# Modulation vectors in blocks of 256 features, layer 1's amid the first feed-forward part, with a third buffer for turned probabilities and the first pair's loads on Pool's queue

## The chip, the cores and the metric

The kernel runs on one core of a Trainium2 chip. The engines are PE (TensorE, the matmuls), DVE (VectorE), ACT (ScalarE), POOL (GpSimd) and SP (SyncE, which here issues most of the DMAs); PEld is PE's loading of weights beside its matmuls. Each engine takes its instructions in the order in which they are queued, and waits at an instruction whose data or buffer isn't ready. The metric is the time of one execution on the device in microseconds (us): the median of several runs.

## What is computed

Two layers of a hybrid backbone over 1024 latent tokens and 256 context tokens of 1024 features. Every layer is an attention part and a feed-forward part, each behind a norm whose shift, scale and gate come from the conditioning vectors c and c_ctx.

```python
def _rms(x, g):
    x32 = x.astype(jnp.float32)
    y = x32 * lax.rsqrt(jnp.mean(x32 * x32, axis=-1, keepdims=True) + EPS)
    return (y * g.astype(jnp.float32)).astype(x.dtype)

def _swiglu(h, wg, wu, wd):
    return (jax.nn.silu(h @ wg) * (h @ wu)) @ wd

# layer 0: Fourier groups beside windowed attention with 8 query and 2 key heads
o = jnp.concatenate([_fourier_mix(f), _window_attention(q, k, v, kc, vc, sink)], axis=-1) @ w_out
# layer 1: 2-D neighbourhood attention with 16 heads and a relative bias
o = _neighbourhood_attention(q, k, v, kc, vc, rel_bias) @ w_out
```

The modulation is, for each layer, SiLU of the conditioning vector times a matrix `ada_w` of 1024 x 6144, plus a bias `ada_b`. The 6144 results are six vectors of 1024: shift, scale and gate of the attention part, then of the feed-forward part. There are two rows: one for the latent tokens, one for the context. The inner width of the feed-forward part is 2816, that is, 22 slices of 128.

## The kernel before

Big matmuls are computed with operands that are split into a high and a low part, three matmuls (high x high, low x high, high x low; `mm3`, lines 74 to 76) in place of one. The stages lie on the span about as follows: head and first projection to 200 us, the Fourier part, attention 0 from 236 to 469, output projection and first feed-forward part to 1530, projection of layer 1 to 1870, attention 1 to 2143, then the second output projection and feed-forward part to the end.

**Modulation.** The weights of the first third of layer 0 come in the head, in eight blocks of 256 features (`ada_block`). A block is 1 MB: one load, matmuls with the conditioning vector as the weight side (32 columns) and 256 features moving, four parts of the contraction side by side in PE's column groups (line 126; called M here), ACT's copy of the four partial rows, two small matmuls that add the parts and turn the rows into columns (line 133; called F), and DVE's addition of the bias. The other five thirds (two of layer 0, three of layer 1) run in attention 0 as `ada_third`: eight loads of 1 MB, four matmuls of 512 features for each (line 149), and a finish: ACT copies the rows, four transposes turn them (line 157), and DVE adds the bias. That makes 40 load steps and 5 finishes, spread over the 78 units of attention by a table (`before`), with a PSUM bank of their own (`psa`). The norm gains for layer 1 follow attention 0.

**Attention.** A `Unit` is one block of 128 queries with its keys. `scores` runs the matmuls, `maxima` (DVE) adds the bias and finds the maximum, `exponents` (ACT) writes the probabilities `pr` and their sum, `normalise` scales them (DVE's reciprocal at line 607, then Pool), and `turn` transposes them in parts of 128 keys into PSUM tiles `pt_ps` (PE, line 616), from where DVE (line 622, the first part) or ACT (line 620, the second) copies them to `prob_t`; the matmuls `po` with the values follow. The parts of a unit are at most two or three PSUM banks wide. `pipeline2` (line 630) goes through the units in pairs: the step for pair b emits its scores, normalises pair b-1 and turns pair b-2. Inside attention the order on PE, DVE, ACT and Pool is the one in which the code emits it (`manual_schedule`); in the other stages a scheduler sets it.

**Feed-forward.** `ffn` (line 855) goes through the slices f in blocks of 3, 3, and eight times 2. `gate_up` takes one f over the chunks of tokens (512, the context's 256, and 512; in the text below C0, CX and C1): matmuls `g_ps` and `u_ps` with the two weights, SiLU, product, and the split into act_hi and act_lo. `down` multiplies a block's slices by w_down and adds the result to x. Each weight, 512 KB, passes through `weights` (line 788): a tile `w_raw` of a pool with **two** buffers, loaded by SP; ACT's cast to `w_hi` (line 794), and DVE's difference `w_lo` (line 795); w_hi and w_lo have four buffers each. A buffer of w_raw comes free when both have been computed.

```python
self.ww, self.ww_cm = pools.open(f"weights{l}", bufs=4)
self.wr, self.wr_cm = pools.open(f"raw{l}", bufs=2)
...
raw = self.wr.tile(shape, F32, name="w_raw")
nc.sync.dma_start(raw, raw_ap)
```

**Attention 1** works through 8 pairs of heads. `load_pair` takes k, q and v of a pair from DRAM into a pool with two buffers; `load_part` issues the loads from SP's queue. In the program they come after all writes of the projection (`v_d` last). Pool's queue loads `mask1` (line 1101) at the head of this stage, clears the bias tables `btab` and adds the mask to them (line 1134).

## Time and profile before

| | |
|---|---|
| time, median of 3 runs (lowest, highest) | 2992.25 us (2988.78, 2996.73) |
| the profiled execution | 2993.83 us |
| its span (first to last instruction) | 2991.7 us |
| mean granted clock of PE | 0.989 |
| DVE, ACT, POOL busy | 46%, 29%, 10% of the span |
| loads of the modulation, 1 MB each (`ada_w`) | 48, median 4.9 us from issue to landing |
| loads of k, 640 KB, and q, 512 KB, in layer 1 | median 10.4 and 16.7 us |

How to read the rows further below. A row of the busy windows has the stretch, its length, then for PE, PEld, DVE, ACT and POOL the busy time with the number of instructions, then PE's granted clock (1.00 is full speed), the mean busy share of the DMA engines, and GB/s. A row of instruction groups has the line, engine, operation, output <- inputs, partitions x elements and count; then busy time in us and the mean of one in ns; then the idle time of the engine just before them and what ended it. A row of waits has the engine, the waiting tile and line, what it waited for, the total in us, how many times, and the longest. A row of the timeline has start and length in us, engine, line, operation, and in brackets the idle time before it with its releaser. A row of DMA issues has the tensors, the issuing queue (SPq is SP's), the count, KB each and the median us from issue to landing. PE's matmuls overlap in the pipeline, so the time from start to start is shorter than one row's length.

### The profile page before, as it was taken

What the parts mean: (1) busy time and instruction counts of PE and PEld (TensorE: products, weight loads), DVE (VectorE), ACT (ScalarE), POOL (GpSimd) and SP (SyncE); (2) the same over time, 40 slices, a digit from 0 to 9 for tenths busy, and PEclk for the clock granted to TensorE, in tenths of its full rate; (3) what the DMA queues carried; (4) which work ended last, traced back from release to release, by engine and by line L of the source; (5) the groups of instructions that cost most, each with busy time, mean ns of one, the idle gap of its engine ahead of it and who ended that gap; (6) DMA issues with size and microseconds to landing.
All of it is one profiled execution on the core that took longest, in us unless ns stands there. A gap on an engine that the chain in (4) does not pass through costs nothing.

```text
span 2991.7 us, 37131 instructions
## 1 busy us (share of the span) xinstructions
PE 2854.2 (95%) x14830; PEld 2288.4 (76%) x14830; DVE 1372.8 (46%) x2510; ACT 863.2 (29%) x1637; POOL 308.6 (10%) x435
## 2 busy tenths in 40 slices
PE   7988889999999999999979999699999999999999
PEld 5875547888888888888857788577677888888887
DVE  5774443533223333333575241466564444444446
ACT  4344443421111111111253231466543111111110
POOL 1112222000000000000130001455210000000000
PEclk9989999999999999999999999899999999999999
DMA  7226554211011101110124332877231111111111
GB/s 273 99 100 231 192 196 160 74 36 43 29 43 35 43 31 41 43 42 30 54 92 131 113 104 86 203 175 174 104 105 43 49 43 43 56 43 53 47 43 71
DMA packets 117212, 267.12 MB, mean 89 GB/s; under 512 B 9232, under 2 KB 67088, under 8 KB 110000
## 3 DMA queue, kind: packets, MB, share of 16 engines
q1 hardware_dynamic: 111920, 252.22, 26.8%
q10 hardware_dynamic: 4176, 8.53, 0.8%
q0 software_dynamic: 944, 4.00, 0.4%
q8 instruction: 117, 1.92, 0.3%
q14 instruction: 55, 0.45, 0.0%
HBM read 223.69 MB, written 41.03 MB: 88 GB/s over the span
## 4 chain that ended last, share of the span: by engine, by line
PE 73%; DVE 5%; ACT 2%; issue 2%; DMA 2%; POOL 1%; SPq 0%; POOLq 0%; ACTq 0%; DVEq 0%
PE d_ps L76 9%; PE d_ps L74 9%; PE d_ps L75 9%; PE u_ps L76 7%; PE u_ps L75 7%; PE u_ps L74 7%; PE g_ps L76 7%; PE g_ps L74 7%; PE g_ps L75 7%; PE pt_ps L616 1%; DVE sm L596 1%; PE po L1185 1%; DVE nrm_t L846 1%; ACT pr L602 1%; POOL pr L608 1%
## 5 line engine op out<-in xcount | busy, mean ns | idle before, releaser
L794 ACT CAST w_hi<-w_raw 128x1024 fp32r<-128x1024 f32 x188 | 195.2, 1049 | 888.8 <-PE d_ps L75 489.8
L897 DVE SCALAR_TENSOR_TENSOR x<-d_ps,mod,x 128x512 f32<-128x512 f32 (+1 forms) x400 | 348.1, 881 | 166.3 <-PE d_ps L76 165.4
L795 DVE TENSOR_TENSOR w_lo<-w_raw,w_hi 128x1024 fp32r<-128x1024 f32 x184 | 224.0, 1224 | 300.6 <-ACT w_hi L794 295.9
L881 DVE TENSOR_TENSOR sg<-sg,u_ps 128x512 f32<-128x512 f32 (+1 forms) x110 | 69.8, 634 | 569.5 <-PE u_ps L76 569.5
L74 PE MATMUL d_ps<-act_hi,w_hi 128*128 128x512 f32 (+1 forms) x880 | 327.6, 373 | 3.5 <-DVE x L897 3.4
L75 PE MATMUL d_ps<-act_lo,w_hi 128*128 128x512 f32 (+1 forms) x880 | 327.6, 372 | 1.3 <-DVE act_lo L883 1.3
L76 PE MATMUL d_ps<-act_hi,w_lo 128*128 128x512 f32 (+1 forms) x880 | 327.7, 372 | 0.0
L602 ACT ACTIVATE pr<-sm,st 128x640 f32<-128x640 f32 (+4 forms) x208 | 162.4, 781 | 224.5 <-DVE st L596 201.5
L74 PEld LDWEIGHTS d_ps<-act_hi,w_hi 128*128 128x128 f32 x880 | 165.6, 188 | 37.4 <-DVE x L897 5.6
L608 POOL TENSOR_SCALAR pr<-pr,st 128x640 f32<-128x640 f32 (+2 forms) x208 | 156.0, 750 | 335.6 <-DVE st L607 207.3
L75 PEld LDWEIGHTS d_ps<-act_lo,w_hi 128*128 128x128 f32 x880 | 165.6, 188 | 32.6 <-DVE act_lo L883 1.8
L76 PEld LDWEIGHTS d_ps<-act_hi,w_lo 128*128 128x128 f32 x880 | 165.6, 188 | 31.2
L74 PE MATMUL u_ps<-o_hi,w_hi 128*128 128x512 f32 (+1 forms) x528 | 189.0, 358 | 0.0
L75 PE MATMUL u_ps<-o_lo,w_hi 128*128 128x512 f32 (+1 forms) x528 | 189.0, 358 | 0.0
L76 PE MATMUL u_ps<-o_hi,w_lo 128*128 128x512 f32 (+1 forms) x528 | 188.9, 358 | 0.0
L74 PE MATMUL g_ps<-o_hi,w_hi 128*128 128x512 f32 (+1 forms) x528 | 188.3, 357 | 0.0
L75 PE MATMUL g_ps<-o_lo,w_hi 128*128 128x512 f32 (+1 forms) x528 | 188.2, 357 | 0.0
L76 PE MATMUL g_ps<-o_hi,w_lo 128*128 128x512 f32 (+1 forms) x528 | 188.2, 357 | 0.0
L616 PE MATMUL pt_ps<-ident,pr 128*128 128x128 f32 x944 | 148.4, 281 | 36.0 <-DVE st L607 16.1
L616 PEld LDWEIGHTS pt_ps<-ident,pr 128*128 128x128 f32 x944 | 105.5, 141 | 68.5 <-DVE pt L622 26.5
L829 POOL TENSOR_TENSOR nrm_ss<-nrm_ss,nrm_sq 128x512 f32<-128x512 f32 (+1 forms) x38 | 48.2, 1268 | 1061.6 <-PE d_ps L76 935.7
L882 ACT CAST act_hi<-sg 128x512 fp32r<-128x512 f32 (+1 forms) x110 | 63.6, 578 | 298.0 <-DVE sg L881 298.0
(263 smaller groups left out, 5892.4 us busy)
## 6 DMA issues: line engine op xcount, KB each, us to landing
ada_w<-ada_w SPq DMA_DIRECT2D x48, 1024.0 KB, 4.9
w_raw<-w_gate SPq DMA_DIRECT2D x44, 512.0 KB, 3.4
w_raw<-w_up SPq DMA_DIRECT2D x44, 512.0 KB, 3.4
w_raw<-w_down SPq DMA_DIRECT2D x44, 512.0 KB, 3.5
k<-k_d SPq DMA_DIRECT2D x32, 640.0 KB, 10.4
w_raw<-w_out SPq DMA_DIRECT2D x32, 512.0 KB, 3.5
w_raw<-w_in SPq DMA_DIRECT2D x24, 512.0 KB, 4.5
q<-q_d SPq DMA_DIRECT2D x16, 512.0 KB, 16.7
```

What stands on the lines that cost most here:

```text
L74: TE.matmul(out, lh, rh, start=first, stop=False)
L75: TE.matmul(out, lh, rl, start=False, stop=False)
L76: TE.matmul(out, ll, rh, start=False, stop=last)
L602: S.activation(self.pr[:, :n], self.sm[:, :n], AF.Exp, bias=st[:, 0:1], scale=-1.0, accum_out=st[:, 1:2])
L608: G.tensor_scalar(self.pr[:, :n], self.pr[:, :n], st[:, 3:4], 0.0, ALU.mult, ALU.add)
L616: TE.transpose(pt[:, b * P:(b + 1) * P], self.pr[:, (b0 + b) * P:(b0 + b + 1) * P], ident)
L794: S.copy(hi, raw)
L795: eng.tensor_tensor(lo, raw, fl(hi), ALU.subtract)
L829: adder(i).tensor_tensor(ss, ss, sq, ALU.add)
L881: V.tensor_tensor(sg[:, :n], sg[:, :n], u_ps[:, :n], ALU.mult)
L882: S.copy(a_hi[:, sl], sg[:, :n])
L897: V.scalar_tensor_tensor(xs, self.shaped(ps[:, :n]), vec(l, 5)[:, dt, v:v + 1], xs, ALU.mult, ALU.add)
```

## The change

- The modulation runs in blocks of 256 features everywhere; `ada_third` and its PSUM bank are gone. Layer 0's blocks 8 to 23 run in attention 0, a load ahead, M and F in turn at the beginning of every step of a pair, from the third on. Their PSUM tile is a `pt_ps`.
- Layer 1's 24 blocks run in the first feed-forward part: a generator `modulation1` that `gate_up` advances for f > 1, by two steps behind the first chunk and one behind each of the others. A block is loaded in two halves of 512 KB, into the two buffers of `w_raw`.
- `pst` of attention 0 has three buffers (as attention 1's has had).
- `turn` goes through a unit's parts from the last to the first, so that ACT's copy comes first and DVE's last; `pipeline2` emits maxima, turn, exponents in place of maxima, exponents, turn. Both attentions share this code.
- In attention 1 each of the two buffers for k, q, v is a pool of its own, and the first pair's seven loads are issued from Pool's queue.

```diff
-    def ada_block(b, xpool, wpool, ptr, name):
-        w = xpool.tile([P, KT, 256], F32, name="ada_w", tag="x8")
-        nc.sync.dma_start(w, io["ada_w0"][b])
+    def ada_block(b, xpool, wpool, ptr, name, parts=1, tag="x8"):
+        l, ct = b // 24, 2 * (b % 24)
+        n = KT // parts
+        ws = [xpool.tile([P, n, 256], F32, name="ada_w", tag=tag) for _ in range(parts)]
+        for i, w in enumerate(ws):
+            nc.sync.dma_start(w, io["ada_w"][b, :, i * n:(i + 1) * n])
         yield
         ps = ptr.tile([P, 512], F32, name=name)
         for i in range(2):
             for q in range(4):
-                TE.matmul(ps[32 * q:32 * q + 32, :256], csil[:, 4 * i + q, :], w[:, 4 * i + q],
+                k = 4 * i + q
+                TE.matmul(ps[32 * q:32 * q + 32, :256], csil[:, k, :], ws[k // n][:, k % n],
                           start=i == 0, stop=i == 1, tile_position=(0, 32 * q))
...
         def turn(self):
-            b0 = 0
-            for s0, sl in self.parts:
+            b0 = self.ncol // P
+            for s0, sl in reversed(self.parts):
                 n = (sl.stop - sl.start) // P
+                b0 -= n
...
                 for u in new[i:i + 1]:
                     u.maxima()
-                    u.exponents()
                 for u in turned[i:i + 1]:
                     u.turn()
+                for u in new[i:i + 1]:
+                    u.exponents()
...
-    pst, pst_cm = pools.open("pst", bufs=2, psum=True)
+    pst, pst_cm = pools.open("pst", bufs=3, psum=True)
...
-    psa, psa_cm = pools.open("psa", bufs=1, psum=True)
...
-    steps = [f for l, s_ in ((0, 1), (0, 2), (1, 0), (1, 1), (1, 2))
-             for f in ada_third(l, s_, xq, aw, psa, pst, "pt_ps")]
-    for i, f in enumerate(steps):
-        before.setdefault(i * 78 // len(steps) + 1, []).append(f)
+    def modulation(ada, i):
+        if i % 2 == 0 and i // 2 + 1 < len(ada):
+            advance(ada[i // 2 + 1], 1)
+        advance(ada[i // 2], 1 + i % 2)
+    ada = [ada_block(b, xq, aw, pst, "pt_ps") for b in range(8, 24)]
+    advance(ada[0], 1)
+    for i in range(2 * len(ada)):
+        before.setdefault(2 * (2 + i), []).append(lambda i=i: modulation(ada, i))
...
                     advance(side, 8)
+                    if f > 1:
+                        advance(extra, 2 if c0 == 0 else 1)
...
+    def modulation1():
+        for b in range(24, 48):
+            yield from ada_block(b, dl.wr, dl.wk, dl.pm, "pmisc", 2, "w_raw")
+            yield
+        ada_gain(1, 1, 2)
+        ada_gain(1, 4, 3)
+    steps = dl.ffn(last, fin0, ((CX, C0, C1), norm1, first_weights), modulation1())
...
-    kp, kp_cm = pools.open("kp1", bufs=2)
+    kps, kp_cms = zip(*(pools.open(f"kp1{i}") for i in range(2)))
...
-            nc.sync.dma_start(dst, src)
+            (nc.sync if pr else G).dma_start(dst, src)
```

Where this moves instructions. **SP in the first feed-forward part**, the loads of slices f = 2 to 5 with the first down block between them. Names ending in a number are single tiles; `w_raw` and the half blocks `ada_w` (128 x 1024) share two buffers. Before:

```order
135 L792 DMA w_raw_5791<-w_gate 128x1024
136 L792 DMA w_raw_5797<-w_up 128x1024
137 L792 DMA w_raw_5970<-w_down 128x1024
138 L792 DMA w_raw_5976<-w_down 128x1024
139 L792 DMA w_raw_5982<-w_down 128x1024
140 L792 DMA w_raw_6252<-w_gate 128x1024
```

Now, at the same place:

```order
111 L772 DMA w_raw_5757<-w_gate 128x1024
112 L772 DMA w_raw_5763<-w_up 128x1024
113 L124 DMA ada_w_5826<-ada_w 128x1024
114 L124 DMA ada_w_5827<-ada_w 128x1024
115 L124 DMA ada_w_5955<-ada_w 128x1024
116 L124 DMA ada_w_5956<-ada_w 128x1024
117 L772 DMA w_raw_5959<-w_down 128x1024
118 L772 DMA w_raw_5965<-w_down 128x1024
119 L772 DMA w_raw_5971<-w_down 128x1024
120 L772 DMA w_raw_6241<-w_gate 128x1024
121 L772 DMA w_raw_6247<-w_up 128x1024
122 L124 DMA ada_w_6380<-ada_w 128x1024
```

Each pair of half blocks stands between two pairs of weights, and takes both raw buffers.

**PE at the end of a slice**, with the last `u_ps` of f = 2 and the beginning of the first down block. Before:

```order
2514 L75 MATMUL u_ps_5916<-o_lo_1664,w_hi_5799 128x512
2515 L76 MATMUL u_ps_5916<-o_hi_1663,w_lo_5800 128x512
2516 L74 MATMUL d_ps_5988<-act_hi_5395,w_hi_5972 128x512
2517 L75 MATMUL d_ps_5988<-act_lo_5396,w_hi_5972 128x512
2518 L76 MATMUL d_ps_5988<-act_hi_5395,w_lo_5973 128x512
```

Now:

```order
2505 L76 MATMUL u_ps_5901<-o_hi_1663,w_lo_5766 128x512
2506 L130 MATMUL pmisc_6310<-ada_w_5955,csil_65 32x256 x4
2507 L130 MATMUL pmisc_6310<-ada_w_5956,csil_65 32x256 x4
2508 L137 MATMUL pmisc_6321<-sel_68,ada_rows_6319 128x2 x2
2509 L74 MATMUL d_ps_5977<-act_hi_5361,w_hi_5961 128x512
2510 L75 MATMUL d_ps_5977<-act_lo_5362,w_hi_5961 128x512
2511 L74 MATMUL d_ps_5988<-act_hi_5361,w_hi_5961 128x512
2512 L75 MATMUL d_ps_5988<-act_lo_5362,w_hi_5961 128x512
```

M and F of a block stand between u_ps and d_ps, whose w_hi_5961 is the cast of w_raw_5959, loaded behind the half blocks that M reads. M and F stand together like this at 12 places, six ahead of a down block and six ahead of the next slice's gate; at the other 12 M stands ahead of the last chunk of a slice and F behind it.

**Pool at the start of attention 1.** Before:

```order
221 L1101 DMA mask1_14255<-mask1 128x896
222 L1207 MEMSET btab0_14257 128x256
223 L1207 MEMSET btab1_14258 128x256
224 L1207 MEMSET btab2_14259 128x256
225 L1207 MEMSET btab3_14260 128x256
226 L1128 DMA btab0_14257<-rel_bias 128x512
```

Now:

```order
221 L1092 DMA mask1_14682<-mask1 128x896
222 L1116 DMA k_14689<-k1_d_85 64x2x1280 x4
223 L1116 DMA q_14688<-q1_d_84 64x2x1024 x2
224 L1199 MEMSET btab0_14684 128x256
225 L1199 MEMSET btab1_14685 128x256
226 L1199 MEMSET btab2_14686 128x256
227 L1199 MEMSET btab3_14687 128x256
228 L1120 DMA btab0_14684<-rel_bias 128x512
```

The loads of k and q stand behind the mask's, and the load of v follows those of the bias.

**ACT in attention 0** (`pr` is the exponent's output, `pt` the target of the copy of a turned part). Before:

```order
288 L602 ACTIVATE pr_3157,st_3155<-sm_3153,st_3155 128x641
289 L620 COPY pt_2941<-pt_ps_3164 128x256
290 L602 ACTIVATE pr_3174,st_3172<-sm_3170,st_3172 128x641
291 L620 COPY pt_2941<-pt_ps_3181 128x256
292 L723 CAST o_hi_1663<-po_3112 128x2x128
```

Now:

```order
294 L596 COPY pt_2946<-pt_ps_3153 128x256
295 L577 ACTIVATE pr_3162,st_3151<-sm_3149,st_3151 128x641
296 L596 COPY pt_2946<-pt_ps_3170 128x256
297 L577 ACTIVATE pr_3179,st_3168<-sm_3166,st_3168 128x641
298 L698 CAST o_hi_1663<-po_3110 128x2x128
299 L133 COPY ada_rows_3198<-pt_ps_3189 128x256
```

Within a unit's turn the copy now stands ahead of the exponent, and the copy of a block's rows stands between two steps.

## The prediction, made before the changed kernel was run

> **What bounds the kernel now.** I read the page's busy shares first, then the chain that ended last, then the windows stage by stage, the waits of PE inside each stage, and single steps on the timeline.

> ```profile
> span 2991.7 us, 37131 instructions
> PE 2854.2 (95%) x14830; PEld 2288.4 (76%) x14830; DVE 1372.8 (46%) x2510; ACT 863.2 (29%) x1637; POOL 308.6 (10%) x435
> PE 73%; DVE 5%; ACT 2%; issue 2%; DMA 2%; POOL 1%; SPq 0%; POOLq 0%; ACTq 0%; DVEq 0%
> 236.00:470.00 234.00, 196.03 (x1381) 116.09 (x1380) 111.06 (x366) 104.99 (x271) 67.13 (x158) 0.99 0.58 206
> 600.00:660.00 60.00, 60.00 (x319) 51.15 (x319) 23.12 (x33) 18.24 (x28) 0.00 (x0) 1.00 0.11 36
> 1380.00:1440.00 60.00, 60.00 (x319) 51.21 (x318) 19.19 (x27) 9.80 (x15) 0.00 (x0) 1.00 0.10 36
> 1892.00:2143.00 251.00, 238.28 (x1793) 181.04 (x1794) 158.78 (x542) 162.20 (x414) 133.52 (x184) 0.99 0.64 151
> ```

> PE bounds the kernel, but unevenly. In a window row the first figure after the length is PE's busy time. The first feed-forward part (600 to 1440) is full to the last hundredth: whatever is added to PE there is paid in full, and so is every wait. Attention 0 (236 to 470) leaves PE idle for 38 us, attention 1 for 12.7 after its start. So the change takes work from a stage with room and puts some into a stage without any.

> **Attention 0.** What PE spends there beside attention itself:

> ```profile
> L149 PE MATMUL ada_ps<-ada_w,csil 128*32 128x512 f32 x320 | 42.2, 604 | 7.5 <-DMA ada_w<-ada_w 7.5
> L157 PE MATMUL pt_ps<-ident,ada_rows 128*128 128x128 f32 x20 | 3.3, 286 | 3.9 <-ACT ada_rows L154 3.9
> PE pt_ps L616 <- DVE st L607: 15.0, 29, 0.6
> PE pt_ps L616 <- ACT pt L620: 5.6, 24, 0.5
> ```

> Gone are 42.2 + 3.3 = 45.5 us of modulation matmuls, with the 7.5 + 3.9 = 11.4 us that PE waited just before them (for the 1 MB loads, and for ACT's copy of the rows). What comes back is 16 blocks. The head of the kernel runs the same block code already:

> ```profile
> 25.91 0.50 PE L133 MATMUL pmisc<-sel,ada_rows 128*128 128x2 f32 x4
> 26.35 1.07 PE L126 MATMUL pmisc<-ada_w,csil 128*32 128x256 f32 x16
> 27.35 0.50 PE L74 MATMUL pq<-w_hi,h_hi 128*128 128x512 f32 x1
> 27.69 0.40 PE L75 MATMUL pq<-w_lo,h_hi 128*128 128x512 f32 x1
> 27.92 0.39 PE L76 MATMUL pq<-w_hi,h_lo 128*128 128x512 f32 x1
> ```

> From start to start a block's main matmuls (M) take 27.35 − 26.35 = 1.00 us and its two small ones (F) 26.35 − 25.91 = 0.44; the first matmul behind them takes 0.34 instead of 0.23, 0.11 more. 16 × 1.44 = 23.0, so the matmuls fall by 22.5 us.

> The turn (ten transposes a step) waits because two PSUM buffers serve three copies and ACT's exponent stands ahead of its copy. One step:

> ```profile
> 273.78 0.42 PE L627 MATMUL s_ps<-kB,q 128*128 128x384 f32 x1
> ...
> 275.04 0.71 PE L616 MATMUL pt_ps<-ident,pr 128*128 128x128 f32 x5
> 276.27 0.52 PE L616 MATMUL pt_ps<-ident,pr 128*128 128x128 f32 x3 [0.52 <-DVE st L607]
> 276.99 0.44 PE L616 MATMUL pt_ps<-ident,pr 128*128 128x128 f32 x2 [0.20 <-ACT pt L620]
> 277.36 1.08 PE L717 MATMUL po<-pt,vt 128*64 128x256 f32 x8
> 1969.75 1.48 PE L616 MATMUL pt_ps<-ident,pr 128*128 128x128 f32 x10
> 1971.16 0.87 PE L1185 MATMUL po<-pt,v 128*64 128x256 f32 x8
> ```

> Here ten transposes last 277.36 − 275.04 = 2.32 us, 0.72 of it waits; in layer 1, which has three buffers already, ten without a wait last 1971.16 − 1969.75 = 1.41. So each 0.72 us of waits goes with 0.91 of time. The waits of 15.0 + 5.6 = 20.6 us are then worth 20.6 × 0.91/0.72 = 26.0. The sum is 22.5 + 11.4 + 26.0 = 60; I give back 0.1 us in each of 40 steps for new waits (M and F take turns in the third buffer), and take **−56**. If the turn waited as before, only 22.5 + 11.4 = 34 would be left; with no new wait at all it is 60. Nothing else binds: DVE's 111 us and ACT's 105 in this stage lie far under what PE keeps.

> **First feed-forward part.** Layer 1's 24 blocks come here, PE's cost for the M alone 24 × 1.00 = 24.0. Where M and F land decides the rest. In 12 blocks M is followed by the last chunk of the same f, with weights already there, and F comes a chunk later: 12 × 0.44 + 24 × 0.11 = 7.9 more, so **+32**. In the other 12, M ends an f, F follows at once, and the next matmul wants weights whose load stands behind M: the half blocks lie in the two buffers through which all weights pass (tag w_raw), so SP can issue the next weight only when M has read its half. The weights of before were far ahead:

> ```profile
> SPq L792 <- DVE w_lo L795: 1685.0, 166, 40.3
> w_raw<-w_gate SPq DMA_DIRECT2D x44, 512.0 KB, 3.4
> w_raw<-w_down SPq DMA_DIRECT2D x44, 512.0 KB, 3.5
> L794 ACT CAST w_hi<-w_raw 128x1024 fp32r<-128x1024 f32 x188 | 195.2, 1049 | 888.8 <-PE d_ps L75 489.8 <-PE g_ps L75 173.7 <-PE u_ps L75 129.9
> L795 DVE TENSOR_TENSOR w_lo<-w_raw,w_hi 128x1024 fp32r<-128x1024 f32 x184 | 224.0, 1224 | 300.6 <-ACT w_hi L794 295.9
> ```

> SP spent 1685 us waiting for buffers to come free, so a load's 3.4 us and a cast's 1.05 were hidden. At these 12 places they are not. M's first half is read after 0.5 us; then 3.4 landing + 1.05 cast + about 0.1 for the hand-overs (an estimate from the gaps between such rows) = 4.55 until the next weight is usable, of which M's second half covers 0.5: 4.05 us from M's end to PE's next big matmul, F's 0.44 inside it. 12 × 4.05 = 48.6. Six of the places go into gate, whose first rows have 0.7 us of matmuls before one needs w_lo, 1.22 after the cast: 6 × 0.5 = 3.0. Two of the other six have three weights for two buffers; the third load starts at 4.55 + 1.22 = 5.8, is cast by 10.3, and PE has eighteen matmuls of 0.23 = 4.1 before it: 10.3 − 4.55 − 4.1 = 1.6 each, 3.2. Together **+55**.

> The third cost is the clock:

> ```profile
> 1496.00:1498.00 2.00, 0.43 (x2) 0.00 (x0) 2.00 (x3) 1.03 (x2) 1.78 (x2) 1.00 0.35 131
> 1500.00:1502.00 2.00, 2.00 (x8) 1.57 (x8) 0.25 (x1) 1.97 (x3) 1.26 (x1) 0.76 0.00 0
> 1502.00:1504.00 2.00, 2.00 (x6) 1.59 (x5) 0.00 (x0) 1.97 (x3) 1.12 (x1) 0.50 0.00 0
> 1504.00:1506.00 2.00, 2.00 (x9) 1.61 (x9) 0.50 (x3) 0.57 (x3) 0.00 (x0) 0.89 0.72 227
> 1498.96 1.05 PE L192 MATMUL pmisc<-ones,nrm_ss 128*128 128x1 f32 x8 [2.53 <-POOL nrm_ss L829]
> 1542.00:1544.00 2.00, 0.54 (x2) 0.48 (x3) 1.28 (x3) 2.00 (x3) 0.00 (x0) 1.00 0.00 0
> ```

> PE waited 2.53 us, and soon afterwards the granted clock (the figure behind the five engines) fell to 0.76, 0.50 and 0.89 in three 2 us windows: 2 × (0.24 + 0.50 + 0.11) = 1.7 us of work lost. Around 1543 PE was busy for 0.54 of 2 us and nothing followed. A wait of about 3.6 us (4.05 less F) is longer than the one that was punished, so I charge 12 × 1.7 = **+20**; the ends are 0 and 20. [...]

> The stage costs 32 + 55 + 20 = 107. The least is 32 + 12 × 3.6 = 75, if hand-overs overlap and the clock stays, the most about 120, if landings are 1 us slower.

> **Start of attention 1.**

> ```profile
> 1825.49 0.61 POOL L1101 DMA_DIRECT2D mask<-mask  x1 [270.98 <-DMA k_d<-qk_lo]
> 1870.81 2.74 SPq L1124 DMA_DIRECT2D k<-k_d  x4
> 1891.01 0.55 PE L627 MATMUL s_ps<-k,q 128*128 128x256 f32 x1 [21.42 <-DMA q<-q_d]
> 1892.00:1898.00 6.00, 6.00 (x26) 4.90 (x26) 4.25 (x14) 3.77 (x9) 2.85 (x4) 0.58 1.07 280
> ```

> PE waits 21.42 us for loads that SP issues at 1870.81, behind its last write of v_d, and then runs six microseconds at clock 0.58 (2.5 lost). Pool's queue issues the mask at 1825.49; the k and q loads now stand right behind it, and their source was written for that mask's wait too. Seven issues on Pool at some 0.6 us each end by 1830; with 40 us before PE arrives at 1869.6, nearly double the longest wait of 21.42, they are there. Pool's memsets and mask sums move back by about 4 us, also with room. I keep 1 us for the hand-over and 1 for the clock: 21.4 + 2.5 − 2 = **−22** (at least 18).

> **Turn order in attention 1.**

> ```profile
> PE pt_ps L616 <- DVE pt L622: 10.0, 22, 0.7
> ```

> The turn now hands out ACT's part first, with no exponent ahead of it, and DVE's last. I take 9 of these 10.0 us: **−9**, with 3 and 11 as the ends, since a wait for DVE may become one for ACT, which is as busy there (162 us to 159).

> **The sum.** −56 + 32 + 55 + 20 − 22 − 9 = +20. The profiled execution took 2993.8 us, 2.1 of it outside the span and untouched, which gives 3013.8; it lay 1.6 above the median of the three runs, so **3012**.

> **The rivals.**

> **The clock holds** (22%). The waits of 3.6 us may not cost a half-speed stretch: the row at 1542 shows PE three quarters idle and no drop. Then +20 becomes 0 and the sum is 0: **2992**, no change. The price that decides: 56 + 22 + 9 − 32 = 55 us are available, 55 / 12 = 4.6 us for each stalled place, all in; above it the kernel is slower. [...]

> **The weights are not late** (10%). If SP got the next weight in ahead of the half blocks, or the four buffers of w_hi already held it, M and F would be all: 24 × 1.44 + 36 × 0.11 = 38.5 in place of 107. −56 − 22 − 9 + 38.5 = −48.5, **2944**. Against it: the rows of SP shown with the change have the half blocks ahead of the weights that PE needs next, and there are just two raw buffers. It decides from the point at which landing and cast take less than the work left between M and that weight's first use; that work is nothing.

> **Attention 0 gives less** (14%). The exponent now comes later on ACT, so the scaled probabilities come later, and the next turn could wait for them instead of for a buffer. Then −34 in place of −56: **3034**. For it speaks only that PE's waits are put down to DVE's small operation at L607, which follows an exponent; against it, ACT's 105 us of 234.

> **The first loads are late anyway** (5%): 22 us are lost, **3034**.

> **All goes better** (7%): the clock holds, each stall is 3.6 us with no extras, attention 0 gives 60, layer 1's turns 11: 75 − 60 − 22 − 11 = −18, **2974**.

> **How the numbers follow.** The forecast has the remaining 42%, with a range of its own from 2998 to 3028. About 0.3%, 9 us, is what a measurement of this kernel can tell from no change: below 2983 is faster, above 3001 slower. Faster: 10 + 7 and a quarter of the 22 = 22%. Same: the rest of the 22 (17) and the low edge of the forecast (8) = 25%. Slower: 53%. The range runs from 2970 to 3040: it leaves out the 10% at 2944 and a few per cent at the top.

> **What would show it.** In the changed kernel's windows between 600 and 1500, PE should be idle some 40 us in twelve pieces of 3 to 4.5 us, each ended by ACT's cast of a weight, and the granted clock should fall behind most of them. Waits before the transposes of attention 0 should fall from 20 us to under 5, and the stage end about 56 us earlier. The first scores of attention 1 should follow the last matmul of the projection within 2 us. PE full from 600 to 1500 would prove the stalls wrong; clock 1.00 behind them, the third cost; a step of attention 0 above 5 us (5.6 in the quoted one), the first term.

## The result, and the profile after

The changed kernel takes **3009.52 us** (median of 4 runs, 3008.44 to 3011.23) beside 2991.1 for the kernel before (four runs, one more than above): a ratio of 1.0059, 95% interval 1.0042 to 1.0077. It is slower by 18 us; forecast were 3012 and a chance of 0.53 for slower.

The head of the page of the changed kernel, and its chain that ended last:

```profile
span 3006.6 us, 38166 instructions
PE 2889.4 (96%) x15290; PEld 2329.1 (77%) x15290; DVE 1381.9 (46%) x2530; ACT 876.2 (29%) x1672; POOL 313.2 (10%) x442
PE 88%; DVE 5%; DMA 3%; ACT 3%; issue 1%; POOL 1%; ACTq 0%; SPq 0%; POOLq 0%; DVEq 0%
```

PE is busy for 35 us more, though five thirds of the modulation are the same work in another form; most of that is work at half clock, as shown below (31.6 us lost to the clock in the feed-forward stage, 1.7 before). The timeline of PE gives the edges of the stages: the first scores of attention 0, the first output projection, layer 1's projection, attention 1's first scores, and the second output projection.

```profile
237.75 0.39 PE L602 MATMUL s_ps<-kA,q 128*128 128x256 f32 x1 [0.24 <-ACT q L651]
406.25 0.80 PE L74 MATMUL d_ps<-o_hi,w_hi 128*128 128x512 f32 x1 [1.42 <-ACT w_hi L774]
1579.12 0.79 PE L74 MATMUL d_ps<-w_hi,o_hi 128*128 128x512 f32 x1
1916.94 0.28 PE L602 MATMUL s_ps<-k,q 128*128 128x256 f32 x1
2162.75 0.50 PE L74 MATMUL d_ps<-h_hi,w_hi 128*128 128x512 f32 x1
```

The same rows in the kernel before (the fourth, at 1891.01, stands in the prediction):

```profile
237.17 0.38 PE L627 MATMUL s_ps<-kA,q 128*128 128x256 f32 x1
468.64 0.50 PE L74 MATMUL d_ps<-o_hi,w_hi 128*128 128x512 f32 x1 [1.42 <-ACT w_hi L794]
1529.37 0.50 PE L74 MATMUL d_ps<-w_hi,o_hi 128*128 128x512 f32 x1 [1.11 <-DVE x L897]
2148.49 0.50 PE L74 MATMUL d_ps<-h_hi,w_hi 128*128 128x512 f32 x1 [1.44 <-ACT w_hi L794]
```

The differences between neighbours are the lengths of the stages (us):

| stage | before | after | difference | forecast |
|---|---|---|---|---|
| attention 0 | 231.5 | 168.5 | -63.0 | -56 |
| output projection and first feed-forward part | 1060.7 | 1172.9 | +112.1 | +107 |
| layer 1's projection, and the wait for the first loads | 361.6 | 337.8 | -23.8 | -20 (the wait, of the 22) |
| attention 1 | 257.5 | 245.8 | -11.7 | -11 (turn order 9, clock 2) |

The four add up to +13.7, and with head and tail the span of the profiled execution is 14.9 us longer; the medians of all runs differ by 18.4. The cost sits where it was forecast. The busy windows of the two attentions and of the feed-forward part, and PE's waits in the latter:

```profile
238.00:406.00 168.00, 162.60 (x1352) 118.20 (x1351) 111.59 (x357) 105.57 (x280) 67.32 (x158) 1.00 0.38 131
600.00:1500.00 900.00, 856.43 (x4523) 705.53 (x4522) 276.51 (x407) 126.42 (x191) 0.00 (x0) 0.96 0.18 61
1917.00:2163.00 246.00, 238.33 (x1806) 180.52 (x1805) 163.84 (x544) 165.75 (x418) 133.78 (x184) 1.00 0.68 156
PE g_ps L74 <- ACT w_hi L774: 18.4, 6, 3.2
PE d_ps L74 <- ACT w_hi L774: 15.6, 6, 2.6
PE pmisc L137 <- ACT ada_rows L133: 9.2, 12, 0.8
```

Twelve waits for ACT's cast of a weight, six into gate and six into down, and twelve short ones for the copied rows, ahead of F: 43.2 us in all, where the windows of before showed PE full. The figure behind the five engines is the granted clock: 0.96 as a mean of 900 us. One of the twelve places, on the timeline of all engines and in windows of 2 us:

```profile
610.52 1.07 PE L130 MATMUL pmisc<-ada_w,csil 128*32 128x256 f32 x16
611.22 5.93 SPq L772 DMA_DIRECT2D w_raw<-w_down  x3
611.95 0.37 ACT L133 COPY ada_rows<-pmisc 128x256 f32<-128x256 f32 x1
612.36 0.61 PE L137 MATMUL pmisc<-sel,ada_rows 128*128 128x2 f32 x4 [0.77 <-ACT ada_rows L133]
614.50 1.04 ACT L774 CAST w_hi<-w_raw 128x1024 fp32r<-128x1024 f32 x1 [2.19 <-DMA w_raw<-w_down]
615.60 0.79 PE L74 MATMUL d_ps<-act_hi,w_hi 128*128 128x512 f32 x1 [2.62 <-ACT w_hi L774]
616.00:618.00 2.00, 2.00 (x6) 1.52 (x6) 1.94 (x2) 0.83 (x1) 0.00 (x0) 0.50 0.14 39
618.00:620.00 2.00, 2.00 (x6) 1.54 (x5) 0.09 (x1) 0.00 (x0) 0.00 (x0) 0.50 0.94 279
620.00:622.00 2.00, 2.00 (x8) 1.60 (x7) 0.91 (x1) 1.04 (x1) 0.00 (x0) 0.75 0.63 213
```

Read it from above. M starts at 610.52. SP issues the weight 0.70 us later, as soon as M's first half has freed a raw buffer. It lands 3.28 us after that; ACT casts it; PE goes on at 615.60. From M's end (one block's 1.00 us) that is 4.08 us; the forecast said 4.05. Then PE works at half its clock for over 5 us, to 621.00 (windows cut at that point stand in the last section).

In attention 0 a step's turn now looks like this, ten transposes without a break, M behind them:

```profile
300.31 1.39 PE L592 MATMUL pt_ps<-ident,pr 128*128 128x128 f32 x10
301.63 1.08 PE L692 MATMUL po<-pt,vt 128*64 128x256 f32 x8
302.65 1.07 PE L130 MATMUL pt_ps<-ada_w,csil 128*32 128x256 f32 x16
303.65 0.44 PE L602 MATMUL s_ps<-kA,q 128*128 128x384 f32 x1
```

From 300.31 to 301.63 are 1.32 us, where it was 2.32.

### The profile page after: what moved, and what is told of

It reads as the page before. It is cut to its first block, busy times and chain, and to the rows that moved or that the text cites. A ratio compares the mean times of both kernels' runs of the same rounds, so it can differ in the third digit from the quotient of the medians.

```text
span 3006.6 us, 38166 instructions
## 1 busy us (share of the span) xinstructions
PE 2889.4 (96%) x15290; PEld 2329.1 (77%) x15290; DVE 1381.9 (46%) x2530; ACT 876.2 (29%) x1672; POOL 313.2 (10%) x442
## 4 chain that ended last, share of the span: by engine, by line
PE 88%; DVE 5%; DMA 3%; ACT 3%; issue 1%; POOL 1%; ACTq 0%; SPq 0%; POOLq 0%; DVEq 0%
PE d_ps L74 9%; PE d_ps L75 9%; PE d_ps L76 9%; PE g_ps L74 7%; PE g_ps L76 7%; PE g_ps L75 7%; PE u_ps L75 7%; PE u_ps L76 7%; PE u_ps L74 7%; PE pt_ps L592 3%; PE po L1177 3%; PE s_ps L602 2%; PE s_ps L603 2%; PE po L692 1%; DMA w_raw<-w_in 1%
## 5 line engine op out<-in xcount | busy, mean ns | idle before, releaser
L74 PE MATMUL d_ps<-act_hi,w_hi 128*128 128x512 f32 (+1 forms) x880 | 334.9, 381 | 19.0 <-ACT w_hi L774 15.6
L75 PE MATMUL d_ps<-act_lo,w_hi 128*128 128x512 f32 (+1 forms) x880 | 333.4, 379 | 1.3 <-DVE act_lo L863 1.3
L76 PE MATMUL d_ps<-act_hi,w_lo 128*128 128x512 f32 (+1 forms) x880 | 327.3, 376 | 0.0
L74 PE MATMUL g_ps<-o_hi,w_hi 128*128 128x512 f32 (+1 forms) x528 | 196.6, 372 | 18.4 <-ACT w_hi L774 18.4
L74 PEld LDWEIGHTS d_ps<-act_hi,w_hi 128*128 128x128 f32 x880 | 169.0, 192 | 55.4 <-ACT w_hi L774 16.1
L75 PEld LDWEIGHTS d_ps<-act_lo,w_hi 128*128 128x128 f32 x880 | 169.2, 192 | 33.0 <-DVE act_lo L863 1.8
L76 PEld LDWEIGHTS d_ps<-act_hi,w_lo 128*128 128x128 f32 x880 | 168.4, 191 | 32.1
L75 PE MATMUL g_ps<-o_lo,w_hi 128*128 128x512 f32 (+1 forms) x528 | 193.2, 366 | 0.0
L76 PE MATMUL g_ps<-o_hi,w_lo 128*128 128x512 f32 (+1 forms) x528 | 192.5, 365 | 0.3 <-DVE w_lo L775 0.3
L859 ACT ACTIVATE sg<-g_ps 128x512 f32<-128x512 f32 (+1 forms) x110 | 61.0, 555 | 440.8 <-PE g_ps L76 440.0
L75 PE MATMUL u_ps<-o_lo,w_hi 128*128 128x512 f32 (+1 forms) x528 | 188.8, 358 | 0.0
L74 PE MATMUL u_ps<-o_hi,w_hi 128*128 128x512 f32 (+1 forms) x528 | 188.6, 357 | 0.0
L76 PE MATMUL u_ps<-o_hi,w_lo 128*128 128x512 f32 (+1 forms) x528 | 188.5, 357 | 0.0
L592 PE MATMUL pt_ps<-ident,pr 128*128 128x128 f32 x944 | 139.0, 278 | 6.8 <-ACT pt L596 3.5
## 6 DMA issues: line engine op xcount, KB each, us to landing
ada_w<-ada_w SPq DMA_DIRECT2D x48, 512.0 KB, 4.0
w_raw<-w_gate SPq DMA_DIRECT2D x44, 512.0 KB, 3.2
w_raw<-w_up SPq DMA_DIRECT2D x44, 512.0 KB, 3.2
w_raw<-w_down SPq DMA_DIRECT2D x44, 512.0 KB, 3.3
w_raw<-w_out SPq DMA_DIRECT2D x32, 512.0 KB, 3.3
w_raw<-w_in SPq DMA_DIRECT2D x24, 512.0 KB, 4.1
```

The source lines that it names most:

```text
L74: TE.matmul(out, lh, rh, start=first, stop=False)
L75: TE.matmul(out, lh, rl, start=False, stop=False)
L76: TE.matmul(out, ll, rh, start=False, stop=last)
L592: TE.transpose(pt[:, b * P:(b + 1) * P], self.pr[:, (b0 + b) * P:(b0 + b + 1) * P], ident)
```

## The experiments

The first question was whether the cost in the feed-forward part comes from the place of the blocks or from the blocks themselves. **Another pace**, with every M in the midst of a slice:

```diff
-                        advance(extra, 2 if c0 == 0 else 1)
+                        two = f < 7
+                        advance(extra, {0: 2, SEQ: 3 if two else 1, 512: int(two)}[c0])
```

> The changed kernel with another pace of layer 1's modulation: every block's main matmuls stand ahead of a chunk whose weights are already there, none at the end of a slice. Theory (the weights that PE needs next were loaded behind the block's matmuls, because both use the two raw buffers): the 12 waits of about 4.1 us and the half clock behind them go, 48 + 31 us, and the 32 us of matmuls stay: 3009.5 - 80 = about 2930 us; PE idle under 5 us between 600 and 1500. Rival 1 (a block costs some 4.7 us wherever it stands, because small fp32 matmuls upset PE or its clock): 3009 us. Rival 2 (with the raw buffers taken by half blocks the weights come late in any place): 2960 to 2990 us.

Measured: **2937.29 us** (2936.71 to 2937.93), a ratio to the kernel before of 0.9817, interval 0.9801 to 0.9834. The windows of this run:

```profile
600.00:1500.00 900.00, 893.73 (x4848) 739.18 (x4848) 318.97 (x470) 155.39 (x244) 20.69 (x17) 1.00 0.19 67
```

PE is idle for 6 us of 900 (the stage ends earlier, so its last 20 us hold norm waits that lay outside before), and no wait for a weight's cast is left. The clock is 1.00. The stage takes 1101.5 us: 71.4 less than in the changed kernel with the same 24 blocks, and 40.8 more than before. So a block costs 40.8 / 24 = 1.70 us where weights are at hand, and 4.67 on the mean of the changed kernel. Of the 40.8, 2.6 are half clock behind waits for the norm at the end of the stage, long after the last block (4.3 us lost to the clock in the whole stage, 1.7 before; how this is summed is said with the filling runs); the matmuls alone come to 38.9, or 1.62 a block. Both rivals fall. The time is 7 us above what was expected: of the 48 us of waits that were to go, F's matmuls fill some 5 and stay, and of the 31 us of clock 27 came back.

**All 40 blocks in attention 0:**

```diff
-    ada = [ada_block(b, xq, aw, pst, "pt_ps") for b in range(8, 24)]
+    ada = [ada_block(b, xq, aw, pst, "pt_ps") for b in range(8, 48)]
...
-        before.setdefault(2 * (2 + i), []).append(lambda i=i: modulation(ada, i))
+        before.setdefault(i * 78 // 80 + 1, []).append(lambda i=i: modulation(ada, i))
...
-    steps = dl.ffn(last, fin0, ((CX, C0, C1), norm1, first_weights), modulation1())
+    steps = dl.ffn(last, fin0, ((CX, C0, C1), norm1, first_weights))
```

> The changed kernel with layer 1's 24 blocks moved back into attention 0, all 40 blocks there. Theory (attention 0 has become PE-bound, so the matmuls of 24 blocks cost there what they take, 24 x 1.44 = 35 us, and the feed-forward part returns to its 1061 us): 3009.5 - 112 + 35 = about 2932 us. Rival (attention 0 was short because the blocks had gone; with two tiles more in each step the three buffers of turned probabilities bring the waits back): 2950 to 2975 us.

Measured: 2948.66 us (2946.23 to 2953.31), 17 above the theory and close to the rival's figure. The feed-forward stage is back at 1060.6 us, as expected; attention 0 takes 217.5, 49 more instead of 35. PE's waits there:

```profile
PE pt_ps L137 <- ACT ada_rows L133: 13.1, 20, 1.2
PE po L692 <- DVE o_lo L700: 2.0, 2, 1.0
```

No transpose waits, so it isn't the three buffers: the waiting line is F, which in half of the steps stands right behind its own M and waits for ACT's copy of the rows. The expectation had the right sum and overlooked this wait. To try that reading, a run with **one block in each step, F of the block before ahead of M** (the rest as in the run with all 40 blocks):

```diff
+    def modulation(ada, j):
+        if j:
+            advance(ada[j - 1], 1)
+        if j + 1 < len(ada):
+            advance(ada[j + 1], 1)
+        advance(ada[j], 1)
...
+    for j in range(len(ada)):
+        before.setdefault(2 * j, []).append(lambda j=j: modulation(ada, j))
```

> All 40 blocks in attention 0, one in each step, with F of the block before ahead of M, so that ACT's copy has a step's time. Theory (the 13.6 us which PE waited in the run with all blocks there came from F right behind its own M): attention 0 from 217.5 to about 204 us, 2935 us, level with the other pace (2937.3) or a little below. Rival (three buffers are too few for five tiles in a step): 2949 us or more.

Measured: 2939.28 us (2936.18 to 2941.01); attention 0 takes 204.9 us, 12.6 less, and the waits for the rows are gone. Its 36.4 us more than in the changed kernel are 1.52 for each of 24 blocks. It is level with the other pace (2937.29): PE is busy for 199.5 of 204 us here, and for 893.7 of 900 there.

**Does the clock fall because PE idles?** Two runs put matmuls without use behind M at the twelve places, so that PE has work while the weight is under way; the sum of them goes to no output.

```diff
-    def ada_block(b, xpool, wpool, ptr, name, parts=1, tag="x8"):
+    def ada_block(b, xpool, wpool, ptr, name, parts=1, tag="x8", fill=0):
...
+        for _ in range(fill):
+            TE.matmul(ps[:, 256:], o_hi[:, 0, :P], o_hi[:, 0, :256], start=True, stop=True)
...
-            yield from ada_block(b, dl.wr, dl.wk, dl.pm, "pmisc", 2, "w_raw")
+            yield from ada_block(b, dl.wr, dl.wk, dl.pm, "pmisc", 2, "w_raw", 28 if b % 4 in (1, 2) else 0)
```

> The changed kernel with 28 matmuls of 128x256 (0.12 us each, 3.3 us) behind a block's main matmuls at the 12 places where PE waits; their result is not used. They need no weight, so the weights land as before, but PE isn't idle. Theory (the half clock follows the idle time): the wait stays as long, the clock stays at 1.00 and the time falls by the lost clock, some 31 us: about 2980 us; granted clock between 600 and 1500 near 1.00 in place of 0.96. Rival (the clock falls for another reason: the 32-column matmuls, or the transfers): 3009 us or more, clock 0.96.

Measured: 2993.73 us (2991.34 to 2997.4), 15.8 below the changed kernel and not 30. The windows:

```profile
600.00:1500.00 900.00, 888.09 (x4944) 740.61 (x4943) 281.12 (x414) 128.79 (x195) 0.00 (x0) 1.00 0.18 63
```

The clock is 1.00, as the theory has it; the time is not. Over the whole stage, in windows of 1 us, I summed PE's busy time times what is missing from a clock of 1.00, and the idle time. In the changed kernel 31.6 us are lost to the clock and 53.5 idle (before: 1.7 and 11.0); in this run 3.4 and 22.9. So 28.2 us of clock are won, as expected. But a fill row lasts 3.61 us, 12 x 3.61 = 43.3, and takes the place of only 53.5 - 22.9 = 30.6 us of idle time: the fill is as long as the wait, and F, which had stood within the wait, comes behind the matmuls that follow it. -28.2 - 30.6 + 43.3 = -15.5, and the stage is 14.1 shorter. I first suspected that a cast comes late behind ACT's copy, which waits for the fill, and tried **20 matmuls instead of 28**:

> The first filling run with 20 matmuls in place of 28 (2.4 us), so that ACT's copy of the rows, which waits for them, is done before the weight lands, and the cast behind it isn't late. Theory: 4.1 us from the end of the main matmuls to the next big one, as in the changed kernel, at full clock: the feed-forward stage falls from 1172.9 by 28 to 33 us, 2977 to 2982 us. Rival (filling gives only the 14 us of the first run, the rest of the loss isn't the clock's): 2994 us.

Measured: 3001.42 us (2997.4 to 3004.88), a miss: the suspicion was wrong. The first of the twelve places, in windows and on PE's timeline:

```profile
612.19 2.65 PE L133 MATMUL pmisc<-o_hi 128*128 128x256 f32 x20
615.36 0.61 PE L139 MATMUL pmisc<-sel,ada_rows 128*128 128x2 f32 x4 [0.52 <-ACT ada_rows L135]
617.47 0.50 PE L74 MATMUL d_ps<-act_hi,w_hi 128*128 128x512 f32 x1 [1.50 <-ACT w_hi L776]
616.00:618.00 2.00, 0.53 (x2) 0.48 (x3) 0.72 (x2) 1.15 (x2) 0.00 (x0) 1.00 0.34 137
618.00:620.00 2.00, 2.00 (x7) 1.53 (x6) 1.70 (x2) 0.94 (x1) 0.00 (x0) 0.61 0.14 27
620.00:622.00 2.00, 2.00 (x7) 1.56 (x6) 0.20 (x1) 0.08 (x1) 0.00 (x0) 0.54 0.85 274
```

With the shorter fill F stands within the wait again, PE idles for 0.52 and 1.50 us around it, and at this place that is enough for the clock to halve again; over the stage 13.4 us are lost. The next weights also came into use a little later: from M's end to the next big matmul 4.6 us pass on the mean of the twelve places, 4.3 in the changed kernel. The less the fill covers, the more clock goes: 3.4, 13.4 and 31.6 us lost with 28, 20 and no matmuls. M and the transfers are the same in all three, so the idle time brings the drop. It doesn't do so every time: with 20 matmuls the clock fell at five of the twelve places; with no filling it fell at all twelve.

**The first pair's loads on SP again:**

```diff
-            (nc.sync if pr else G).dma_start(dst, src)
+            nc.sync.dma_start(dst, src)
```

> The changed kernel with the first pair's seven loads on SP's queue again. Theory: PE waits some 21 us at the start of attention 1, and works for 6 us at about 0.58 of the clock: 3009.5 + 22 = about 3032 us. Rival (the early writes of k and q and the two pools would have brought the loads early on SP too): 3010 us.

Measured: 3030.03 us (3028.04 to 3032.6), 20.5 above the changed kernel. PE's first scores in attention 1:

```profile
1941.05 0.55 PE L602 MATMUL s_ps<-k,q 128*128 128x256 f32 x1 [21.46 <-DMA q<-q_d]
```

The wait of before is there again to within 0.04 us (21.42). Splitting the pool into two isn't what brings the loads early; the queue is.

**The old order of the turn, three buffers kept:**

```diff
-            b0 = self.ncol // P
-            for s0, sl in reversed(self.parts):
+            b0 = 0
+            for s0, sl in self.parts:
...
                     u.maxima()
+                    u.exponents()
                 for u in turned[i:i + 1]:
                     u.turn()
-                for u in new[i:i + 1]:
-                    u.exponents()
```

> The changed kernel with the old order of the turn in both attentions: a unit's first part first, and the exponents ahead of the turn; three buffers stay. Theory (the order is worth what attention 1 lost, 9 to 12 us there; in attention 0 the third buffer does most): attention 1 from 245.8 to about 256 us, attention 0 from 168.5 to 169 to 175; together 3019 to 3026 us. Rival (the order does nothing, attention 1's 12 us come from the loads being there): 3010 us.

Measured: 3024.49 us (3022.34 to 3026.42). Attention 0 takes 175.3 us (6.8 more), attention 1 252.9 (7.1 more, where 9 to 12 had been expected), the other stages within 0.5 us of the changed kernel. PE's waits in attention 1 of this run, and of the changed kernel:

```profile
PE pt_ps L591 <- DVE pt L597: 10.6, 22, 0.7
```

```profile
PE pt_ps L592 <- ACT pt L596: 3.5, 16, 0.5
PE pt_ps L592 <- DVE pt L598: 0.3, 1, 0.3
```

The 10 us of before are back, under the same releaser; the new order leaves 3.8, now nearly all for ACT.

**Two buffers, with the new order:**

```diff
-    pst, pst_cm = pools.open("pst", bufs=3, psum=True)
+    pst, pst_cm = pools.open("pst", bufs=2, psum=True)
```

> The changed kernel with two buffers for turned probabilities in attention 0, in place of three; the blocks' M and F go through the same two. Theory (the buffer brings most of the 26 us that the transposes gained): attention 0 from 168.5 to 190 to 205 us, 3031 to 3046 us. Rival (the order of the turn alone does it): 3010 us.

Measured: 3029.57 us (3025.18 to 3030.63). Attention 0 takes 188.4 us, 19.9 more; its waits are for ACT now:

```profile
PE pt_ps L592 <- ACT pt L596: 8.1, 32, 0.3
PE pt_ps L137 <- ACT q L651: 1.9, 8, 0.2
```

It falls just short of both ranges that were expected, at the side of the theory: the third buffer is worth about three times the order in attention 0, for transposes and blocks together, which share it. The two buffers cost more than these waits say (8.1 + 1.9 of 19.9 us). PE's busy time in the stage is 8.9 us longer too, 171.7 in place of 162.9; that this comes from transposes that start anew behind each wait is likely by the step quoted in the prediction (0.72 us of waits went with 0.91 of time), but isn't shown.

## Why the prediction was right, step by step

- **Attention 0, -56; measured -63.0.** The sum of its terms was 60, and 4 were given back for new waits. These didn't come: on `pt_ps` of the transposes PE waits 0.4 us in the whole stage. The transposes' term, 26.0, is close to what the two runs give when added, 6.8 for the order and 19.9 for the buffer; that the two add up is an assumption, and the 19.9 include waits of the blocks' own tiles. Two stretches at half clock in the stage before (255.2 to 258.6, behind a wait of 1.52 us for modulation weights, and 456.6 to 460.0), 1.7 us each, weren't in the sum and went too.
- **Feed-forward, matmuls, +32 beside the F within the waits (12 x 0.44 = 5.3).** Right: by the prediction's own prices all 24 blocks in the open would be 38.5; with the other pace they measured 38.9.
- **Feed-forward, waits, +55.** The mechanism was right to the place and the count, six into gate and six into down. Over the twelve places, read like the one quoted above, 4.05 us pass on the mean from M's end to the next big matmul ahead of down, and 4.5 ahead of gate: 6 x 4.05 + 6 x 4.5 = 51. The 3.2 us for three weights didn't show: at half clock PE reached the third one no sooner than its cast. In the run with 28 filling matmuls, at full clock, the waits for the third weight are there (0.74 us at 622.13 and 0.88 at 765.86).
- **Feed-forward, clock, +20.** Right in kind, too small, and beyond the upper end that the prediction gave it: between 600 and 1500, where the twelve places lie, the clock costs 27.4 us and before nothing, so 2.3 us a place and not 1.7. The price came from a row with one stretch of 3.41 us at half clock; here five places had one such stretch and seven had two. (The rest of the 31.6 us was lost at the two ends of the stage.) The rival in which the clock holds is refuted by the 0.50 in the windows of the result; that it is the idle time that brings the drop is shown by the filling runs (3.4, 13.4 and 31.6 us lost to the clock with 28, 20 and no matmuls). PE's idle time at the place quoted in the result is 0.77 + 2.62 us; at the same place of the short filling run 0.52 + 1.50 us were followed by the half clock too.
- **First loads, -22: right.** 22.2 in that stage by the run on SP (360.0 to 337.8), and 20.5 in the time. Of it, the share of the clock, forecast at 1.5 us inside attention 1, shows as 0.6 there (246.4 to 245.8).
- **Turn order in attention 1, -9; measured -7.1.** 3.5 us of waits for ACT have taken the place of part of those for DVE, as the lower end allowed for. The stage as a whole gained 11.7, which with these 7.1 and the 0.6 for the loads leaves 4.0 that the prediction has no term for. Some 2.4 of them are two waits at the end of the stage before, 0.93 for `h_lo` and 1.44 for a weight's cast, which the changed kernel doesn't have; why they went, no run shows.

The errors went both ways. In the profiled executions 7.0, 3.8 and 0.7 us more than forecast were gained in the other three stages, and 5.1 more were lost in the feed-forward part, where a wait that was too long in the sum met a clock that was too cheap. With 1.2 us at head and tail that leaves some 5 us (3013.8 forecast for the profiled execution, 3008.4 measured). The median lay 1.6 us below the profiled execution before and lies 1.1 above it now, which brings the total to within 3 of the forecast. So the closeness is luck in part; what each term of the sum rests on was seen in the runs.

## What to carry to other kernels

Extra loads that share a weight pool of two buffers are not priced by their own work: the operation that frees the buffer becomes a gate for the next weight, and whatever stands between it and that weight's first use must be longer than landing plus cast (4.4 us from issue to first use at the place quoted, 611.22 to 615.60). Placing the same blocks ahead of a chunk whose weights are already there took 72 us off the changed kernel and made a kernel that is 1.8% faster than the one before. A wait on a full PE cost more than its length here: the clock behind it added 2.3 us on the mean of the twelve places.

## What the runs showed of the hardware

```profile
614.17:617.58 3.41, 1.99 (x5) 1.60 (x6) 1.95 (x2) 2.09 (x2) 0.00 (x0) 0.50 0.30 120
617.58:621.00 3.42, 3.42 (x10) 2.65 (x9) 0.51 (x1) 0.99 (x1) 0.00 (x0) 0.50 0.85 252
621.00:624.41 3.41, 3.41 (x16) 2.75 (x15) 1.93 (x2) 1.10 (x2) 0.00 (x0) 1.00 0.45 162
760.94:764.36 3.42, 3.42 (x8) 2.70 (x9) 2.34 (x2) 1.05 (x1) 0.00 (x0) 0.50 0.38 139
764.36:767.77 3.41, 3.41 (x16) 2.78 (x15) 1.22 (x1) 1.05 (x1) 0.00 (x0) 1.00 0.60 168
```

At these places less than a step of idle time was followed by a drop, and a longer idle time was not always. Two places of the run with 20 filling matmuls, and the first place of the run with 28:

```profile
836.88:840.29 3.41, 2.02 (x11) 1.51 (x11) 1.80 (x3) 2.46 (x3) 0.00 (x0) 1.00 0.31 126
840.29:843.70 3.41, 3.41 (x10) 2.64 (x9) 0.81 (x1) 0.00 (x0) 0.00 (x0) 0.50 0.71 197
901.73:905.14 3.41, 2.48 (x20) 2.19 (x18) 0.62 (x2) 0.51 (x2) 0.00 (x0) 1.00 0.84 282
905.14:908.55 3.41, 2.45 (x11) 2.01 (x12) 2.42 (x2) 1.96 (x2) 0.00 (x0) 1.00 0.07 22
614.80:618.21 3.41, 1.79 (x9) 1.40 (x8) 1.23 (x1) 2.25 (x3) 0.00 (x0) 1.00 0.28 109
618.21:621.63 3.42, 3.18 (x16) 2.38 (x15) 1.39 (x2) 0.71 (x2) 0.00 (x0) 1.00 0.71 242
```

At the first, 1.39 us of idle time within one step (3.41 - 2.02) were followed by a step at 0.50. At the second the idle time is longer, 0.93 + 0.96 = 1.89 us, but spread over two steps, and the clock stayed at 1.00. In that run the five places with a drop had 1.18 to 1.85 us of idle time within one step, the other seven at most 1.00. No limit follows from it, since in the third pair 1.62 us within one step were followed by a clock of 1.00. What decides is open.
